# Second layer of a four-layer hybrid block: k projected two heads ahead, and a mixer's last three steps spread over ten steps of the gates

## The chip, the core and the metric

The kernel runs on one core of one Trainium2 chip. The core's engines run side by side and each takes its own instructions in order: TensorE (PE, matmuls; PEld is its weight load), VectorE (DVE), ScalarE (ACT), GpSimd (POOL) and SyncE (SP), which issues nearly all of the DMAs here. The metric is the device time of one execution in microseconds (us); less is better. Matmul results land in PSUM, 8 banks of 128 x 512 f32; everything else lives in SBUF.

## What is computed

Four layers over 1040 tokens (16 meta tokens and 1024 others) of width 1024: attention with a sliding window (layers 0 and 3), mLSTM (layer 1) and HGRN2 (layer 2). Each does RMS norm, an input projection, its mixer, a gate and an output projection that is added to the residual. The change is in the second layer alone (`kind == 1`). Cut to that layer:

```python
def mlstm_branch(u, w_in, conv_w, conv_b, gate_bias, h_gain, w_out, valid):
    q, k, v, ig, fg, og, z = _split(u @ w_in, B_SIZES)      # 8 heads, dk 128, dv 256
    qk = silu(causal_conv(concat([q, k]), conv_w, conv_b))  # 4 taps over the tokens
    ...
    h = mlstm_chunkwise(qh, kh * 128 ** -0.5, vh, log_i, log_f)   # blocks of 128 tokens
    h = sigmoid(og) * h
    h = rmsnorm(h, h_gain)                                  # per head
    return (h * silu(z)) @ w_out

def step(carry, inp):              # one head, one block of 128 tokens
    C, n, m = carry
    ...
    D = where(causal, a[t] - a[s] + li[s], -inf)
    qk = (q_ @ k_.T) * exp(D - m_t)
    num = w_inter * (q_ @ C) + qk @ v_
    den = w_inter * (q_ @ n) + qk.sum(-1)
    h = num / maximum(abs(den), exp(-m_t))
    C_new = w_old * C + (w_s * k_).T @ v_
```

## The kernel before

**Numbers.** Everything is f32 to its full precision: an operand is split into a high and a low part (`split`, lines 194 to 196: ACT rounds to fp32r at L195, DVE takes the rest at L196), and each product is three matmuls, high by high, high by low and low by high. Weights are fetched in two halves of 128 x 512 (`weights`, L207, on SP's queue) and split in the same way into the tiles `wh` and `wl`, of which there are three each; there are two raw landing tiles `wr`.

**Steps.** The program is one long list of steps, each `[cost, function, prefetch]`. The cost is in units near a nanosecond of ideal matmul time; it only serves to place steps. PE executes them exactly in the order of the list. The order on ACT, DVE, POOL and SP is made by the framework's scheduler from the order of the list and its own model of time; `hi(...)` lets a step's instructions go ahead of those listed up to 40 places earlier. A step's `prefetch` (the weights) is put out 12,000 units of cost ahead of the step (`LOOKAHEAD`). `weave(a, b)` mixes two lists so that both advance by the same share of their cost; `flat` strings lists together; `later` puts a step so many units behind a list's start.

**Projections.** `proj` (L231) makes one 128-wide piece of q, k, output gate `og` or gate `z` for all tokens: three chunks of 400, 384 and 256 tokens, four steps to a chunk, six matmuls to a step, so 72 matmuls. `proj_v` (L281, and L277 for the meta tokens) makes v of a head, block by block. `proj_out` (L326) multiplies a head's result by its output weights and adds to the residual `x` on DVE (L329). It first splits its input by `ysplit` steps of cost 0.

**What follows a chunk of q or k** (`conv_proj`): ACT copies PSUM to `t` (L956) and makes the last tap (L959), DVE adds three taps (L961), then a sigmoid (ACT L454, L455, L456, L458, DVE L457) and a product (DVE L965 or L967). q lives in a pool of two tiles, k in a row of the eight `r` rows, which it shares with the two result rows of each head.

**The mixer of a head** (`mixer`) has nine blocks b and four steps to a block. `s1(b)` (PE L1009, L1011): q by k, the decay matrix E on DVE (L1013, from rows `rw` fetched by SP at L990 one block ahead, three tiles) and ACT (L1015), W = E * qk (DVE L1019), splits of V, W, q and k. `s2(b)`: the numerator, W by V and q by the carried state (PE L997, `po<-Vh,Wh` and `po<-Ch,qwh`), then the division on ACT and DVE. `s3(b)`: the state's update (PE L997 `pa<-Vh,kwh`, DVE L1062 or L1064 into C, then C's split into Ch and Cl). `s4(b)`: the transpose of the result into the rows R["h"] (PE L1073, DVE L1075). The list of a mixer is s1(0); s1(1), s2(0), s3(0); s1(2), s2(1), s3(1), s4(0); and so on, with costs 320, 714, 357 and 214. Its last three steps, `rest`, are s2(8), s4(7) and s4(8).

**The order of the layer.** `body` starts with q0, k0, q1 and the gates' scalar rows. Then, for h = 0 to 5: the mixer of head h but for its last three steps, woven with q(h+1), k(h+1), v(h+1) (h = 0 has no q: q1 is done); `rest` woven with the first six steps of `gates(h)`; the other steps of `gates(h)`, which are og's two projections and the first of z's, with the norm's sums; z's second projection `zg[h][1]`; the output projection `oc[h]`. Mixer 6 is woven with q7, k7, v7, and mixer 7, headed by the three steps held back from mixer 6, follows at once with gates(6) and zg[6][1] beside it. Then come the rest of mixer 7 with gates(7), and zg[7][1]; oc[6] and oc[7] run beside the next layer's head.

Of the kernel before, what the change touches and what calls it, by code (L numbers as in the profile page):

```python
# [32 lines left out]

B_COLS = 96
LOOKAHEAD = 12000.0
TAIL_LAG = 600.0
PRIO = 40
ROWS, TMPS, RAWS, YS = 8, 6, 2, 3
# [19 lines left out]
def weave(a, b):  # L58

    ta, tb = sum(x[0] for x in a) + 1e-9, sum(x[0] for x in b) + 1e-9  # L60
    out, i, j, ca, cb = [], 0, 0, 0.0, 0.0
    while i < len(a) or j < len(b):
        if j >= len(b) or (i < len(a) and ca / ta <= cb / tb):
            ca += a[i][0]
            out.append(a[i])
            i += 1
        else:
            cb += b[j][0]
            out.append(b[j])
            j += 1  # L70
    return out


def flat(groups):
    return [x for grp in groups for x in grp]


def outs(groups):

    first, out = groups[0]  # L80
    out = list(out)
    for splits, grp in groups[1:]:
        out.insert(len(out) - Y_EARLY, splits[0])
        out.insert(len(out) - Y_LAST, splits[1])
        out += grp
    return first, out


def later(steps, *events):

    k, t = 0, 0.0
    for delay, step in events:
        while k < len(steps) and (t < delay or steps[k][0] == 0.0):
            t += steps[k][0]
            k += 1
        steps.insert(k, step)
        t += step[0]
        k += 1
# [15 lines left out]
def hybrid_kernel(ctx: ExitStack, tc: tile.TileContext, ins, out, layers=(0, 1, 2, 3)):  # L114
# [134 lines left out]
    def proj_v(srcs, evac, kind="v"):  # L249

        st = {}
        nc = 256 if kind == "v" else 272
        pieces, k = [], 0
        for src in srcs:
            n = src.shape[-1] // nc
            pieces.append((k, n, src))
            k += n

        groups = []
        for blocks in CHUNK_BLOCKS:  # L260
            grp = []
            for b in blocks:
                c0, cn = blk(b)
                for i, (k0, kn, src) in enumerate(pieces):
                    def pre(i=i, src=src):
                        st[i] = weights(src, kind)

                    def fn(b=b, c0=c0, cn=cn, i=i, k0=k0, kn=kn):
                        if i == 0:
                            st["a", b] = psj()  # L270
                        acc = st["a", b]
                        wh, wl = st[i]
                        for kk in range(kn):
                            k = k0 + kk
                            if b == 0:
                                for m in (wh, wl):
                                    pe.matmul(acc[:48, :nc], um[0][:, k, :], m[:, kk, :],  # L277
                                              start=(k == 0 and m is wh), stop=(k == KT - 1 and m is wl))
                            else:
                                for j, (a, m) in enumerate(((uh, wh), (uh, wl), (ul, wh))):  # L280
                                    pe.matmul(acc[:cn, :nc], a[:, k, c0 : c0 + cn], m[:, kk, :],  # L281
                                              start=(k == 0 and j == 0), stop=(k == KT - 1 and j == 2))
                        if i == len(pieces) - 1:
                            evac(acc, b, c0, cn)

                    grp.append([(2 if b == 0 else 3) * kn * nc * MM, fn, pre if b == 0 else None])
            groups.append(grp)
        return groups
# [172 lines left out]
    def gate_proj(src, o, chunks=CHUNKS, scale=None):  # L461
        rs = {}

        def early(n, c0, cn):
            rs[n] = tmp()
            scale.fetch(rs[n], c0, cn)

        def evac(acc, n, c0, cn):
            cs = slice(c0, c0 + cn)
            z = acc[:, :cn]  # L470
            if scale is not None:
                z = rs[n][:, :cn]
                v.tensor_tensor(z, z, acc[:, :cn], op=ALU.mult)
            a = sigmoid_from(z, cn)
            v.tensor_tensor(a[:, :cn], a[:, :cn], z, op=ALU.mult)
            v.tensor_tensor(o()[:, cs], o()[:, cs], a[:, :cn], op=ALU.mult)

        return proj(src, evac, chunks, None if scale is None else early)
# [384 lines left out]
    def layer_b(i, j, fin):  # L863
# [78 lines left out]
        def conv_proj(src, mt, mul, key):  # L942
            prev = [None, None]

            def evac(acc, n, c0, cn):
                conv = R["conv"]
                raw = tmp()
                if n == 0:
                    if mt < 8:
                        R[key] = R["mix"].tile([P, T], F32, tag="q", name=nm("q"), bufs=2)  # L950
                    else:
                        R[key] = row()
                    v.memset(raw[:, 0:3], 0.0)
                else:
                    v.tensor_copy(raw[:, 0:3], prev[0][:, prev[1] : prev[1] + 3])
                s.copy(raw[:, 3 : 3 + cn], acc[:, :cn])  # L956
                prev[:] = [raw, cn]
                y = R[key][:, c0 : c0 + cn]
                s.activation(y, acc[:, :cn], AF.Identity, bias=conv[:, mt, 4:5], scale=conv[:, mt, 3:4])  # L959
                for q in (2, 1, 0):  # L960
                    v.scalar_tensor_tensor(y, raw[:, q : q + cn], conv[:, mt, q : q + 1], y,  # L961
                                           op0=ALU.mult, op1=ALU.add)
                a = sigmoid_from(y, cn)
                if mul == 1.0:
                    v.tensor_tensor(y, y, a[:, :cn], op=ALU.mult)  # L965
                else:
                    v.scalar_tensor_tensor(y, y, mul, a[:, :cn], op0=ALU.mult, op1=ALU.mult)  # L967

            return proj(src, evac)

        def v_evac(h):
            def f(acc, b, c0, cn):
                R["v", h, b] = V = vtile()
                put_v(V, acc, b, cn)
                if h == 0:
                    gate_evac(acc, b, cn)
                g.memset(V[:cn, 256:258], 1.0)
            return f
# [110 lines left out]
        def og_proj(h):  # L1089
# [20 lines left out]
            def stat(n, c0, cn):  # L1110
                def fn():
# [6 lines left out]
                    for c in range(2):  # L1118
# [8 lines left out]
        qg = {h: conv_proj(win[8 * h], h, 1.0, ("q", h)) for h in range(8)}  # L1127
        kg = {h: conv_proj(win[8 * h + 1], 8 + h, 128 ** -0.5, ("k", h)) for h in range(8)}
        gsrc = [ins["b_wv0"][j][:, 272 * a : 272 * b] for a, b in ((0, 3), (3, 6), (6, 8))]
        vg = {h: proj_v([win[8 * h + 2], win[8 * h + 3]], v_evac(h)) if h else proj_v(gsrc, v_evac(0), "g") for h in range(8)}  # L1130
        og = {h: og_proj(h) for h in range(8)}
        zg = {h: [gate_proj(win[8 * h + 6 + c], lambda h=h, c=c: R["h", h, c]) for c in range(2)] for h in range(8)}
        oc = {h: proj_out(wout[2 * h], wout[2 * h + 1], lambda k, h=h: R["h", h, k], CHUNKS,
                          fin if h == 7 else None, h == 6) for h in range(8)}

        def gates(h):
            g0, g1, stats = og[h]
            tail = flat(zg[h][0])
            for n in (2, 1, 0):
                later(tail, (7000.0, stats[n]))  # L1140
                tail = g0[n] + g1[n] + tail
            return tail
# [5 lines left out]
        body = flat(qg[0]) + flat(kg[0]) + flat(qg[1])  # L1148
        later(body, (GATE_LAG, gate_turn(2)), (0.0, [0.0, gate_rows, None]), (GATE_COLS, [18 * 30, gate_cols, None]))
        for h in range(8):  # L1150
            mx = mixer(h)
            mx, rest = mx[:-3], mx[-3:]
            if h < 7:
                body += weave(mx, (flat(qg[h + 1]) if h else []) + flat(kg[h + 1]) + flat(vg[h + 1]))
                if h < 6:
                    body += weave(rest, gates(h)[:6]) + gates(h)[6:] + flat(zg[h][1]) + flat(outs(oc[h]))
                else:
                    held = rest
            else:
                body += weave(held + mx, gates(6) + flat(zg[6][1]))  # L1160
        body += weave(rest, gates(7)[:6]) + gates(7)[6:] + flat(zg[7][1])
        return head, body, oc[6], oc[7]

    def layer_c(i, j, fin):
# [288 lines left out]
        for h in range(8):  # L1453
# [11 lines left out]
            for r in range(1, 5):  # L1465
                mx += weave(main[r], last)
                last = [[TAIL_LAG, lambda: None, None]]
                if r == 1:
# [19 lines left out]
    for pos, i in enumerate(layers):  # L1488
# [10 lines left out]
        if i % 3 == 0:  # L1499
            head, body, oa, ob = layer_a(i, i // 3, tail is None, i == 3, fin, norm if tail is None else None)  # L1500
        elif i % 3 == 1:
            head, body, oa, ob = layer_b(i, i // 3, fin)
        else:
            head, body, oa, ob = layer_c(i, i // 3, fin)
# [42 lines left out]
    for n, (cost, fn, pre) in enumerate(steps):  # L1547
        while k < len(steps) and (k <= n or ahead < LOOKAHEAD):
            if steps[k][2]:
# [117 lines left out]
```

## Time and profile before

| | us |
|---|---|
| median of 3 runs | 2602.28 (2600.02 to 2602.58) |
| the profiled execution | 2599.31 |
| its span, first to last instruction | 2597.5 |
| PE busy in the span | 2541.0 |
| DVE busy | 2034.6 |
| ACT busy | 1744.6 |
| the second layer, from the first projection of q to the last steps of its gates | about 510 to 1530 |

Busy times are sums of records; a matmul's record lasts longer than the distance to the next one, so PE counts as busy from the first of a run of matmuls until the last has left the array. PEclk is the share of full clock that TensorE was granted. Waits are inferred from semaphores and name the last thing to arrive. A row of the timeline has start, duration, engine, line, operation, tiles, shapes and, in brackets, the idle time of that engine just before, with what ended it.

### The profile page before, as it was taken

What the parts mean: (1) busy time and instruction counts of PE and PEld (TensorE: products, weight loads), DVE (VectorE), ACT (ScalarE), POOL (GpSimd) and SP (SyncE); (2) the same over time, 40 slices, a digit from 0 to 9 for tenths busy, and PEclk for the clock granted to TensorE, in tenths of its full rate; (3) what the DMA queues carried; (4) which work ended last, traced back from release to release, by engine and by line L of the source; (5) the groups of instructions that cost most, each with busy time, mean ns of one, the idle gap of its engine ahead of it and who ended that gap; (6) DMA issues with size and microseconds to landing.
All of it is one profiled execution on the core that took longest, in us unless ns stands there. A gap on an engine that the chain in (4) does not pass through costs nothing.

```text
span 2597.5 us, 55485 instructions
## 1 busy us (share of the span) xinstructions
PE 2541.0 (98%) x20646; PEld 2488.2 (96%) x20646; DVE 2034.6 (78%) x5602; ACT 1744.6 (67%) x4675; POOL 244.2 (9%) x572
## 2 busy tenths in 40 slices
PE   8999999989999999999999999999999999999999
PEld 8899999989999999999999999999999998999999
DVE  7897898785757576767677788978888988887886
ACT  8766766576565656565657757877675857867772
POOL 0321231000000000000000000001000000321320
PEclk9999999999999999999999999999999999999999
DMA  5223212022222212121211111111111113212112
GB/s 157 63 66 94 57 43 69 30 51 56 43 50 45 52 46 53 45 50 49 50 49 43 55 43 43 34 34 34 34 42 34 35 51 93 64 47 77 56 42 77
DMA packets 103344, 140.27 MB, mean 54 GB/s; under 512 B 15369, under 2 KB 58514, under 8 KB 103074
## 3 DMA queue, kind: packets, MB, share of 16 engines
q1 hardware_dynamic: 103074, 136.73, 19.2%
q8 instruction: 162, 2.65, 0.4%
q14 instruction: 108, 0.88, 0.1%
HBM read 121.83 MB, written 4.27 MB: 49 GB/s over the span
## 4 chain that ended last, share of the span: by engine, by line
PE 61%; DVE 14%; ACT 9%; DMA 4%; issue 2%; SPq 0%; POOL 0%; DVEq 0%; ACTq 0%
PE pj L231 29%; PE pj L326 14%; PE pj L281 8%; DMA rw<-rowsd 2%; DVE wl L196 2%; PE po L997 1%; PE po L773 1%; PE pt L755 1%; ACT Sm L737 1%; DVE Sm L734 1%; ACT wh L195 1%; ACT X L1291 1%; PE pj L277 1%; PE pa L997 1%; DVE x L329 1%
## 5 line engine op out<-in xcount | busy, mean ns | idle before, releaser
L231 PE MATMUL pj<-uh,wh 128*128 128x256 f32 (+2 forms) x2688 | 903.6, 336 | 6.9 <-ACT uh L401 6.4
L231 PE MATMUL pj<-ul,wh 128*128 128x256 f32 (+2 forms) x2688 | 865.3, 322 | 0.3
L231 PE MATMUL pj<-uh,wl 128*128 128x256 f32 (+2 forms) x2688 | 864.9, 322 | 0.0
L231 PEld LDWEIGHTS pj<-uh,wh 128*128 128x128 f32 x2688 | 509.0, 189 | 14.6 <-ACT uh L401 6.4
L231 PEld LDWEIGHTS pj<-ul,wh 128*128 128x128 f32 x2688 | 509.4, 189 | 4.4 <-DVE ul L196 0.8
L231 PEld LDWEIGHTS pj<-uh,wl 128*128 128x128 f32 x2688 | 508.0, 189 | 0.0
L196 DVE TENSOR_TENSOR wl<-wr,wh 128x512 fp32r<-128x512 f32 (+1 forms) x338 | 234.2, 703 | 72.0 <-ACT wh L195 69.4
L326 PE MATMUL pj<-yh,wh 128*128 128x384 f32 (+2 forms) x768 | 253.4, 330 | 9.9 <-DVE x L329 8.3
L329 DVE TENSOR_TENSOR x<-x,pj 128x384 f32<-128x384 f32 (+2 forms) x480 | 233.9, 507 | 32.9 <-PE pj L326 31.7
L195 ACT CAST wh<-wr 128x512 fp32r<-128x512 f32 (+1 forms) x338 | 203.3, 614 | 78.7 <-PE pj L326 31.0
L326 PE MATMUL pj<-yh,wl 128*128 128x384 f32 (+2 forms) x768 | 246.3, 321 | 0.0
L326 PE MATMUL pj<-yl,wh 128*128 128x384 f32 (+2 forms) x768 | 246.3, 321 | 0.0
L281 PE MATMUL pj<-wh,uh 128*128 128x256 f32 (+1 forms) x768 | 222.8, 290 | 0.0
L281 PE MATMUL pj<-wl,uh 128*128 128x256 f32 (+1 forms) x768 | 216.3, 282 | 0.0
L281 PE MATMUL pj<-wh,ul 128*128 128x256 f32 (+1 forms) x768 | 215.9, 281 | 0.0
L737 ACT ACTIVATE Sm<-Sm,s 128x257 f32<-128x257 f32 (+2 forms) x272 | 131.1, 483 | 87.7 <-DVE s L734 85.2
L740 POOL TENSOR_TENSOR Sm<-Sm,s 128x512 f32<-128x512 f32 (+2 forms) x136 | 139.4, 1025 | 404.9 <-DVE s L739 389.6
L458 ACT ACTIVATE t<-t 128x384 f32<-128x384 f32 (+2 forms) x240 | 118.2, 493 | 64.5 <-DVE t L457 63.5
L195 ACT CAST yh<-r 128x384 fp32r<-128x384 f32 (+2 forms) x120 | 56.9, 478 | 154.8 <-PE pj L326 138.0
L326 PEld LDWEIGHTS pj<-yh,wh 128*128 128x128 f32 x768 | 144.7, 188 | 13.9 <-DVE x L329 10.4
L326 PEld LDWEIGHTS pj<-yl,wh 128*128 128x128 f32 x768 | 144.9, 189 | 0.7 <-DVE yl L196 0.2
L281 PEld LDWEIGHTS pj<-wh,uh 128*128 128x128 f32 x768 | 144.7, 188 | 0.6
(323 smaller groups left out, 5704.0 us busy)
## 6 DMA issues: line engine op xcount, KB each, us to landing
wr<-in_b_win SPq DMA_DIRECT2D x124, 256.0 KB, 2.8
wr<-in_a_win SPq DMA_DIRECT2D x80, 256.0 KB, 2.7
wr<-in_c_win SPq DMA_DIRECT2D x64, 256.0 KB, 3.0
wr<-in_a_wout SPq DMA_DIRECT2D x32, 256.0 KB, 2.8
rw<-rowsd SPq DMA_DIRECT2D x64, 128.0 KB, 4.3
wr<-in_b_wout SPq DMA_DIRECT2D x32, 256.0 KB, 2.8
t<-t SPq DMA_DIRECT2D x100, 48.0 KB, 1.9
cs<-in_rope SPq DMA_DIRECT2D x11, 400.0 KB, 3.5
```

Of the source, the lines that this page charges most:

```text
L195: s.copy(h, src)
L196: v.tensor_tensor(l, src, h.bitcast(F32), op=ALU.subtract)
L231: pe.matmul(acc[:, :cn], a[:, k, :], b[:, k, c0 : c0 + cn], start=(k == 0 and i == 0), stop=(k == KT - 1 and i == 2))
L277: pe.matmul(acc[:48, :nc], um[0][:, k, :], m[:, kk, :], start=(k == 0 and m is wh), stop=(k == KT - 1 and m is wl))
L281: pe.matmul(acc[:cn, :nc], a[:, k, c0 : c0 + cn], m[:, kk, :], start=(k == 0 and j == 0), stop=(k == KT - 1 and j == 2))
L326: pe.matmul(acc[:, :cn], a[:, k, mc], b, start=(k == 0 and i == 0), stop=(k == 1 and i == 2))
L329: v.tensor_tensor(x[:, m, c0 : c0 + cn], x[:, m, c0 : c0 + cn], acc[:, :cn], op=ALU.add)
L458: s.activation(a[:, :cn], a[:, :cn], AF.Exp)
L734: v.tensor_tensor_reduce(Sm[:nq, u, :nk], S[:nq, u, :nk], R["masks"][:nq, P + mo : P + mo + nk], rq, sinks[u], ALU.add, ALU.min, st[:nq, u ...
L737: s.activation(Sm[:nq, u, : nk + 1], Sm[:nq, u, : nk + 1], AF.Exp, scale=-1.0, bias=st[:nq, u : u + 1], accum_out=den[:nq, u : u + 1])
L740: g.tensor_tensor(Sm[:nq, :, :nk], Sm[:nq, :, :nk], den[:nq].rearrange("p (u c) -> p u c", c=1).to_broadcast([nq, 2, nk]), op=ALU.mult)
L997: pe.matmul(acc, a[x0], c[x1][:, :258], start=(start and i == 0), stop=(stop and i == 2))
```

## The change

Three things, all in `layer_b`. k of head h+2 takes the place of k of head h+1 beside mixer h; beside mixer 0 both k1 and k2 are projected, and beside mixer 6, where no k is left, z's second projection of head 5. That moves `zg[5][1]` from ahead of mixer 6 to beside it, and `oc[5]` from ahead of mixer 6 to behind it. The rest of a mixer is woven with the first ten steps of the gates, and an empty step of 600 units is put ahead of it, which does nothing but shift its place in the weave.

```diff
+REST_LAG, REST_STEPS = 600.0, 10
...
             if h < 7:
-                body += weave(mx, (flat(qg[h + 1]) if h else []) + flat(kg[h + 1]) + flat(vg[h + 1]))
+                fill = flat(qg[h + 1]) if h else flat(kg[1])
+                fill += flat(kg[h + 2]) if h < 6 else flat(zg[5][1])
+                body += weave(mx, fill + flat(vg[h + 1]))
                 if h < 6:
-                    body += weave(rest, gates(h)[:6]) + gates(h)[6:] + flat(zg[h][1]) + flat(outs(oc[h]))
+                    n, gs = REST_STEPS, gates(h)
+                    body += weave([[REST_LAG, lambda: None, None]] + rest, gs[:n]) + gs[n:]
+                    if h < 5:
+                        body += flat(zg[h][1]) + flat(outs(oc[h]))
                 else:
+                    body += flat(outs(oc[5]))
                     held = rest
             else:
                 body += weave(held + mx, gates(6) + flat(zg[6][1]))
-        body += weave(rest, gates(7)[:6]) + gates(7)[6:] + flat(zg[7][1])
+        n, gs = REST_STEPS, gates(7)
+        body += weave([[REST_LAG, lambda: None, None]] + rest, gs[:n]) + gs[n:] + flat(zg[7][1])
```

## The prediction

> **What bounds the kernel now.** I read the page's first part, then what PE waited for inside the second layer, then that layer cut into stages.
>
> ```profile
> PE 2541.0 (98%) x20646; PEld 2488.2 (96%) x20646; DVE 2034.6 (78%) x5602; ACT 1744.6 (67%) x4675; POOL 244.2 (9%) x572
> ```
> ```profile
> PE po L997 <- ACT Ch L195: 5.5, 5, 2.0
> PE po L997 <- DVE Cl L196: 3.6, 7, 1.1
> PE po L997 <- ACT Wh L195: 3.2, 1, 3.2
> PE po L997 <- DVE Wl L196: 0.4, 1, 0.4
> ```
> ```profile
> 541.00:570.00 29.00, 22.36 (x125) 21.11 (x124) 23.11 (x72) 22.61 (x62) 0.20 (x2) 0.82 0.13 32
> 570.00:596.00 26.00, 26.00 (x223) 26.00 (x221) 19.13 (x68) 16.14 (x54) 0.65 (x5) 1.00 0.23 42
> 596.00:612.00 16.00, 13.56 (x87) 13.11 (x86) 7.71 (x26) 6.69 (x20) 1.02 (x7) 0.89 0.49 74
> 676.00:729.00 53.00, 53.00 (x402) 52.80 (x401) 41.48 (x135) 36.07 (x105) 0.78 (x7) 1.00 0.32 53
> 729.00:744.00 15.00, 14.06 (x104) 13.62 (x103) 7.61 (x24) 6.90 (x20) 0.68 (x5) 1.00 0.48 64
> 862.00:877.00 15.00, 13.76 (x102) 13.35 (x102) 7.21 (x24) 7.04 (x20) 0.76 (x7) 1.00 0.30 62
> 995.00:1010.00 15.00, 14.39 (x106) 13.95 (x105) 7.70 (x25) 7.59 (x23) 0.68 (x5) 1.00 0.37 63
> 1127.00:1142.00 15.00, 14.44 (x107) 14.00 (x106) 7.94 (x25) 7.17 (x21) 0.86 (x7) 1.00 0.35 63
> 1259.00:1275.00 16.00, 15.72 (x116) 15.43 (x116) 8.66 (x27) 8.67 (x23) 1.34 (x10) 1.00 0.35 72
> 1391.00:1406.00 15.00, 14.99 (x112) 14.45 (x112) 8.80 (x30) 7.76 (x22) 0.55 (x3) 1.00 0.25 79
> 1406.00:1460.00 54.00, 54.00 (x374) 53.81 (x373) 44.63 (x143) 44.94 (x127) 0.00 (x0) 1.00 0.15 48
> ```
>
> PE sets the time: 2541.0 of 2597.5 us busy. The change removes no matmul, so it can only win where PE stands still. In the second layer all such waits are of one line, s2's products (12.7 us in 14 waits), and the stages place them. The first number of a row is its length and the second PE's busy time. Mixer 0's first blocks (541 to 570) lose 6.64 us at a granted clock of 0.82. The ends of mixers 0 to 5 lose 2.44, 0.94, 1.24, 0.61, 0.56 and 0.28, together 6.07. The body of mixer 1 (676 to 729) loses nothing, nor does the end of mixer 6 or mixer 7.
>
> How a run of matmuls really goes, and so what a step costs, is in its starts, not its durations:
>
> ```profile
> 533.90 0.34 PE L231 MATMUL pj<-ul,wh 128*128 128x400 f32 x1
> 534.08 0.35 PE L231 MATMUL pj<-uh,wl 128*128 128x400 f32 x1
> ...
> 596.39 0.28 PE L281 MATMUL pj<-wl,uh 128*128 128x256 f32 x1
> 596.51 0.28 PE L281 MATMUL pj<-wh,ul 128*128 128x256 f32 x1
> ```
> ```profile
> 549.31 4.00 PE pj L231 x12
> 560.69 3.52 PE pj L231 x12
> 639.89 14.33 PE pj L231 x96
> ```
>
> A 400 column matmul takes 0.18 us of PE, one of 256 columns 0.12. The 96 matmuls of the last piece are a projection (72) and a chunk of 256 (24), so a projection is 14.33 - 24 x 0.12 = 11.45 us. A record outlasts its slot by 0.16 us (0.28 - 0.12), so each wait is longer by that than the windows show. In mixer 0, 12 matmuls that should take 2.2 us took 4.00 and 3.52: 1.8 + 1.3 us lost to the lowered clock. Mixer 0's start thus costs 6.64 + 4 x 0.16 + 3.1 = **10.4 us**. The ends cost 6.07 + 10 x 0.16 = 7.7, plus up to 0.11 x 16 = 1.8 of clock behind mixer 0: **7.7 to 9.4 us**.
>
> **Part 1: the rest of a mixer is spread.** Why an end stalls, shown at mixer 2:
>
> ```profile
> 869.36 0.35 DVE L1013 SCALAR_TENSOR_TENSOR E<-rw,bcol,caus 128x128 f32<-128x128 f32 x1 [2.99 <-DMA rw<-rowsd]
> 869.63 0.48 DVE L1064 SCALAR_TENSOR_TENSOR C<-C,rw,pa 128x258 f32<-128x258 f32 x1
> ...
> 870.28 1.14 ACT L195 CAST wh<-wr 128x512 fp32r<-128x512 f32 x2
> ...
> 871.32 0.41 ACT L195 CAST Ch<-C 128x258 fp32r<-128x258 f32 x1
> ...
> 871.78 0.39 PE L997 MATMUL po<-Ch,qwh 128*128 128x258 f32 x1 [0.79 <-ACT Ch L195]
> ...
> 872.14 0.42 DVE L196 TENSOR_TENSOR Cl<-C,Ch 128x258 fp32r<-128x258 f32 x1
> ...
> 872.62 0.39 PE L997 MATMUL po<-Cl,qwh 128*128 128x258 f32 x1 [0.45 <-DVE Cl L196]
> ```
>
> On DVE the update of C stands behind an E that waits 2.99 us for its row's DMA, and on ACT C's cast stands behind two weight casts. s2(8) is the next thing on PE's list after the last of the mixer, so PE waits. In the new weave the empty step is 600 of 600 + 714 + 214 + 214 = 34% of the list. Ten steps of the gates are 8 x 1000 + 2 x 960 units, and three of them are 30%, four 40%: s2(8) comes behind four steps, which are a whole chunk, 24 x 0.18 = 4.4 us of PE. The largest end stall is 2.44 + 0.32, so the cover suffices at all six ends. s4(7) and s4(8) follow the eighth and ninth step; who reads them last is og's third chunk, which starts behind the sixteenth, so nothing new is late. PE's work and its order beyond are the same, and no DMA is moved. Bounds: 3 us, if the scheduler lets the gates' own work into ACT and DVE ahead of C and half or more of the wait comes back; 9.4 at most. I take **8.5**, near the upper end, because the cover is larger than every wait.
>
> **Part 2: k2 beside mixer 0.** What is late at its start:
>
> ```profile
> 545.10 0.15 DVE L1019 TENSOR_TENSOR W<-E,pm 16x16 f32<-16x16 f32 x1
> ...
> 545.55 0.47 ACT L956 COPY t<-pj 128x400 f32<-128x400 f32 x1
> ...
> 547.21 0.29 ACT L195 CAST Wh<-W 128x128 fp32r<-128x128 f32 x1
> ...
> 555.98 0.42 DVE L1062 COPY C<-pa 128x258 f32<-128x258 f32 x1
> ...
> 558.16 0.40 ACT L195 CAST Ch<-C 128x258 fp32r<-128x258 f32 x1
> ```
>
> The copy at 545.55 is that of q1's first chunk, whose 400 column matmuls ended on PE at 534.4: ACT and DVE run 11 us behind with the convolutions of k0 and q1. W is ready at 545.25 and its cast comes at 547.21, behind that work; C, at 555.98, is cast at 558.16.
>
> The mixer's list is 12,946 units without its rest. s2(0) stands at 640 of them (4.9%), s3(0) at 1354 (10.5%), s2(1) at 2031 (15.7%). The fill grows by one projection, 11.45 us, so s2(0) moves back by 0.56 us, and between s3(0) and s2(1) there is 5.2% x 11.45 = 0.60 us more. That alone takes 1.2 us off the two stalls. During k1 only k2's weights are now prepared, where before both pieces of v1 were:
>
> ```profile
> L196 DVE TENSOR_TENSOR wl<-wr,wh 128x512 fp32r<-128x512 f32 (+1 forms) x338 | 234.2, 703 | 72.0 <-ACT wh L195 69.4
> L195 ACT CAST wh<-wr 128x512 fp32r<-128x512 f32 (+1 forms) x338 | 203.3, 614 | 78.7 <-PE pj L326 31.0
> ```
>
> Two halves fewer are 1.2 us of ACT and 1.4 of DVE out of the queues that are late: 1.2 more. Of the 3.1 us of clock I credit a third, 1.1, since the first gap only shrinks. Bounds for the start: nothing (the queues stay as late), and all 10.4. I take **3.5**, nearer the lower bound, because the backlog itself is not touched.
>
> [...]
>
> What k2 puts back: its own three chunks of convolution on ACT and DVE while they are still late. Lower bound nothing: mixer 1 with q, k and v beside it, the very same mix, loses nothing in 53 us. Upper bound is the slower rival below. I take **-1**, near mixer 1's row. Its two weight DMAs join SP's queue ahead of some `rw` fetches; mixer 1 carries the same load, so nothing is added.
>
> **Part 3: the seams.** Later k's keep the shape of their mixers, k is only a head older, and at most six of the eight rows are held (h5 twice, h6 twice, k6, k7). Beside mixer 6 the lighter zg[5][1] stands for k7. Mixer 6 now follows gates(5) at once; mixer 7 followed mixer 6 at once before, at 0.01 us lost, so 0. oc[5] now follows mixer 6, and its first product needs two splits from queues that are late by a mixer's end: 0 to 1.24 us (the ends of mixers 1 to 5), I take **-0.5**. Its second half of weights must wait for v7 to leave a `wh` tile: two casts and a subtraction, 2 x 0.61 + 0.70 = 1.9 us, hidden by the eight products ahead of it, 24 x 0.18 = 4.4 us; uncovered it would cost those 1.9.
>
> **Sum.** 8.5 + 3.5 - 1 - 0.5 = 10.5 us. Against the profiled execution's own 2599.31 (its span is 2597.5) that is 2588.8; the runs' median stands 3.0 us above that execution, so 2602.28 - 10.5 = **2592**. The bounds of the terms that remain likely give it 2587 to 2597.
>
> **The rivals.**
> - *Only the ends gain.* The start's stalls stay whole, since the backlog is what sets them: 8.5 - 0.5 = 8, 2594.5. For it: W waits on ACT's queue, not on PE's order. Against: two weight splits leave that queue.
> - *Mixer 0 heals wholly*, as mixers 1 to 5 run without a loss: 8.5 + 10.4 = 19, 2583. Against: those start behind an output projection, with empty queues.
> - *No change that can be measured.* ACT and DVE are ordered by the scheduler, not by the weave, and it was this order that put an E and weight casts ahead of C; it may do so again with the gates' work. The ends then give 3, the start 1.2, and the seams take 1.2 and 1: 2 us, 2600.
> - *Slower.* The 11 us of lag does not drain, since k1 and k2 together bring six chunks of convolution, and blocks 2, 3 and 4 of mixer 0 stall as block 1 did (2.0 + 1.1 of wait, 0.3 of records, 1.3 of clock: 4.7 each). The ends gain 8.5, the start nothing, the seams lose 0.5: 3 x 4.7 - 8 = 6 us, 2608. It decides from the second such block on. Against it: from 570 to 596 mixer 0 loses nothing, at closer steps than the change gives it.
>
> **Chances.** Forecast 0.45, only the ends 0.14, healed 0.13, no change 0.16, slower 0.12. About 0.2%, 5.2 us, is what a measurement of this kernel can tell from no change: faster 0.72, same 0.16, slower 0.12. The range, 2583 to 2602, leaves out the slower case and the far end of the healed one.
>
> **What would show it.** Waits of `po` on Ch and Cl at the ends of mixers 0 to 5 should be gone (6.07 us of idle under 1), with s2(8) behind a chunk of L231. Mixer 0's first 29 us should lose 3 to 6 us instead of 6.64 and the stretch with k2 under 2; the steps of mixer 0 should come as evenly as those of mixer 1. The seams show as idle before oc[5]'s first L326. The prediction is wrong if the ends still wait, or if mixer 0 loses more than now.

## The result and the profile after

The changed kernel takes 2585.14 us (median of 6 runs, 2580.66 to 2586.18), the kernel before 2598.73 in its six runs by now. The ratio is 0.9943, with a 95% interval of 0.993 to 0.9956: 14.8 us less by the ratio, 13.6 by the medians. The forecast was 10.5 us less. The profiled execution took 2586.18 us against 2599.31, 13.1 less.

The chain of work that ended last brackets the second layer by the output projections of the layer before it and its own, which run beside the next layer's head. First column start, second length in us. Before:

```profile
451.75 20.51 PE pj L326 x141
...
1531.37 20.44 PE pj L326 x140
```

After (all lines of the code are one or a few higher):

```profile
454.66 20.52 PE pj L327 x141
...
1519.19 20.42 PE pj L327 x140
```

From one to the other it is 1079.62 us before and 1064.53 after: the second layer is 15.1 us shorter, and the untouched first layer happened to end 2.9 us later in this execution. Totals of work are as before:

```profile
PE 2536.4 (98%) x20646; PEld 2486.1 (96%) x20646; DVE 2034.8 (79%) x5602; ACT 1740.8 (67%) x4675; POOL 244.5 (9%) x572
```

The layer cut into stages, with mixer 0's first blocks, its later ones, its end, the end of mixer 1, and the seam of mixer 6 with oc[5] behind it (length, then PE's busy time; the third number from the right is the granted clock):

```profile
541.00:570.00 29.00, 23.86 (x149) 22.74 (x148) 24.12 (x71) 23.61 (x63) 0.20 (x2) 0.94 0.15 42
570.00:606.00 36.00, 36.00 (x289) 35.84 (x288) 29.83 (x99) 26.44 (x79) 0.58 (x5) 1.00 0.22 45
606.00:622.00 16.00, 16.00 (x112) 15.96 (x111) 6.69 (x21) 7.26 (x20) 0.68 (x5) 1.00 0.46 76
...
733.00:748.00 15.00, 15.00 (x117) 15.00 (x116) 7.36 (x26) 5.96 (x19) 1.06 (x8) 1.00 0.44 41
...
1303.00:1370.00 67.00, 67.00 (x506) 66.80 (x505) 49.57 (x156) 43.62 (x126) 1.03 (x9) 1.00 0.21 48
1370.00:1396.00 26.00, 26.00 (x169) 25.66 (x168) 17.70 (x44) 6.96 (x18) 0.31 (x1) 1.00 0.18 61
```

What PE still waited for in the layer, but for one wait of 0.2 us in a norm (us in total, times, longest):

```profile
PE po L998 <- ACT Wh L196: 2.1, 1, 2.1
PE po L998 <- ACT Ch L196: 1.7, 1, 1.7
PE po L998 <- DVE Cl L197: 0.7, 1, 0.7
PE po L998 <- DVE Wl L197: 0.7, 1, 0.7
```

All waits at the ends are gone, the four at mixer 0's start are left (5.2 us where 6.7 were), k2's stretch and both seams lose nothing. The clock's mean in the first 29 us rose from 0.82 to 0.94. Windows miss what a matmul's record covers, 0.16 us of each wait, so I also summed, for every matmul, its distance to the next start above the median distance of its line, tiles and width: 541 to 570 us went from 12.2 to 8.3, the end of mixer 0 from 4.5 to 0.2, and all from 612 to 1540 from 14.8 to 8.5. That is 14.6 of the 15.1 us.

Why the ends no longer wait, at mixer 0 in the timeline after:

```profile
610.96 0.35 DVE L1014 SCALAR_TENSOR_TENSOR E<-rw,bcol,caus 128x128 f32<-128x128 f32 x1 [2.70 <-DMA rw<-rowsd]
611.23 0.48 DVE L1065 SCALAR_TENSOR_TENSOR C<-C,rw,pa 128x258 f32<-128x258 f32 x1
...
612.92 0.41 ACT L196 CAST Ch<-C 128x258 fp32r<-128x258 f32 x1
...
613.74 0.42 DVE L197 TENSOR_TENSOR Cl<-C,Ch 128x258 fp32r<-128x258 f32 x1
...
616.75 0.28 PE L998 MATMUL po<-Vh,Wh 128*128 128x258 f32 x1
...
617.23 0.28 PE L998 MATMUL po<-Cl,qwh 128*128 128x258 f32 x1
```

The queue is not cured: E still holds DVE for 2.70 us in front of C. But Cl is ready at 614.16 and its product comes at 617.23, 3.1 us later, because og's first chunk, 24 matmuls from 612.26 on, now stands ahead of s2(8).

### The profile page after: what moved, and what is told of

The parts are those of the page before. It is cut to its first block, busy times and chain, and to the rows that moved or that the text cites. A ratio compares the mean times of both kernels' runs of the same rounds, so it can differ in the third digit from the quotient of the medians.

```text
span 2584.4 us, 55470 instructions
## 1 busy us (share of the span) xinstructions
PE 2536.4 (98%) x20646; PEld 2486.1 (96%) x20646; DVE 2034.8 (79%) x5602; ACT 1740.8 (67%) x4675; POOL 244.5 (9%) x572
## 4 chain that ended last, share of the span: by engine, by line
PE 61%; DVE 14%; ACT 10%; DMA 2%; issue 2%; SPq 0%; POOL 0%; DVEq 0%; ACTq 0%; POOLq 0%
PE pj L232 27%; PE pj L327 14%; PE pj L282 9%; PE po L998 2%; DVE wl L197 1%; ACT Sm L738 1%; DVE Sm L735 1%; PE po L774 1%; PE pt L756 1%; PE pa L998 1%; ACT X L1299 1%; ACT wh L196 1%; PE pj L278 1%; DVE x L330 1%; DVE X L1297 1%
## 5 line engine op out<-in xcount | busy, mean ns | idle before, releaser
L232 PE MATMUL pj<-uh,wh 128*128 128x384 f32 (+2 forms) x2688 | 903.8, 336 | 6.7 <-ACT uh L402 6.2
L232 PE MATMUL pj<-ul,wh 128*128 128x384 f32 (+2 forms) x2688 | 864.9, 322 | 0.3
L232 PE MATMUL pj<-uh,wl 128*128 128x384 f32 (+2 forms) x2688 | 864.4, 322 | 0.0
L232 PEld LDWEIGHTS pj<-uh,wh 128*128 128x128 f32 x2688 | 508.6, 189 | 14.6 <-ACT uh L402 6.5
```

The lines of the kernel that those rows point to most:

```text
L232: pe.matmul(acc[:, :cn], a[:, k, :], b[:, k, c0 : c0 + cn], start=(k == 0 and i == 0), stop=(k == KT - 1 and i == 2))
```

## The experiments

All ratios are to the kernel before, with 95% intervals; the changed kernel has 0.9943. An interval is 5.7 to 7.8 us wide, so ratios alone do not tell most of these kernels from the changed one. The length of the second layer in the trace, taken between the same two matmuls as in the section above, is free of what the other layers add. It is one execution of each kernel, so differences of a few tenths say nothing:

| run | second layer, us | less than before |
|---|---|---|
| before | 1079.6 | |
| the changed kernel | 1064.5 | 15.1 |
| only the spread | 1070.0 | 9.6 |
| only the order of k | 1071.5 | 8.2 |
| ten steps, no empty step | 1071.4 | 8.2 |
| seams left | 1065.1 | 14.6 |
| mixer 0: 1200 and 1000 units | 1062.1 | 17.5 |
| fewer taps | 1059.7 | 19.9 |
| mixer 0: 2200 units ahead | 1064.1 | 15.5 |
| two subtractions on GpSimd | 1067.0 | 12.7 |
| rows in four pieces | 1066.5 | 13.1 |
| the same, with 900 and 600 units | 1065.2 | 14.5 |
| 900 and 600 units alone | 1065.8 | 13.8 |

### Each part alone

Only the spread of the rest (the kernel before, with `weave([[REST_LAG, lambda: None, None]] + rest, gs[:n]) + gs[n:]` at both places):

> Only the rest of a mixer is spread (empty step of 600, ten steps of the gates); k, zg[5][1] and oc[5] stay where they were. Theory A (the two parts add up; the ends are worth about 10 us by the trace, 6.07 us of idle with the records' overlap and the clock behind mixer 0): 9 to 10.5 us under the kernel before, ratio near 0.9963, no wait of L997's line at the ends, mixer 0's start as before (6 to 7 us idle in 541 to 570). Rival B (the longer fill of mixer 0 is what relieved mixer 0's end): the end of mixer 0 still waits 2 us, 5 to 6 us gained, ratio 0.998.

Measured: **0.9959** (0.9946 to 0.9971), 10.7 us by the ratio, 9.6 by the layer's length. Waits of PE in the layer, but for one of 0.3 us in a norm:

```profile
PE po L998 <- ACT Wh L196: 3.1, 1, 3.1
PE po L998 <- ACT Ch L196: 1.8, 1, 1.8
PE po L998 <- DVE Cl L197: 1.1, 1, 1.1
PE po L998 <- DVE Wl L197: 0.4, 1, 0.4
```

One of each: these are mixer 0's first blocks, as in the kernel before. All six ends are healed by the spread alone, mixer 0's too, so theory A holds and rival B falls.

Only the order of k, zg[5][1] and oc[5]:

```diff
-REST_LAG, REST_STEPS = 600.0, 10
+REST_LAG, REST_STEPS = 600.0, 6
...
-body += weave([[REST_LAG, lambda: None, None]] + rest, gs[:n]) + gs[n:]
+body += weave(rest, gs[:n]) + gs[n:]
```

> Only the order of k, zg[5][1] and oc[5]; the rest of a mixer is woven with six steps of the gates and no empty step, as before. Theory A: mixer 0's start gains 3 to 4 us, the ends of mixers 0 to 5 still wait 0.3 to 2.4 us each; 4 us under before, ratio near 0.9985. Rival B: mixer 0's end heals too, with 8 us under before, ratio 0.997. Rival C (k2 costs beside mixer 0 what it gains): ratio 1.000.

Measured: **0.9971** (0.996 to 0.9982), 7.5 us by the ratio, 8.2 by the layer's length: rival B's size. In the waits neither text holds whole. The start has the changed kernel's waits, and the ends still wait, as theory A has it. At the end of mixer 0, 603 to 615 us:

```profile
PE po L998 <- ACT Ch L196: 0.6, 1, 0.6
PE po L998 <- DVE Cl L197: 0.5, 1, 0.5
```

where before it was 2.0 and 0.5 us with a clock of 0.89. With k2 beside it, mixer 0's end is like that of any other mixer. By the layer's length the two parts alone make 17.7 us and together 15.1. The 2.6 us that are in both are mixer 0's end: summed by distances between starts, as above, it loses 4.5 us in the kernel before and 1.8 here. Beside the spread the order of k is thus worth 5.5 us by the layer's length, and 4.1 by the ratios, whose intervals overlap.

### Which part of the spread carries it

The changed kernel without the empty step: `weave(rest, gs[:n])`, ten steps of the gates kept.

> The changed kernel without the empty step of 600 units: ten steps of the gates, but s2(8) stays the first thing behind the mixer. Theory A (the cover is the chunk of og ahead of s2(8), and the number of steps is nothing): the ends wait as before, time as the kernel with k alone, ratio to before near 0.9985. Rival: the wider spread of s4(7) and s4(8) carries part of the gain: 0.996.

Measured: **0.9965** (0.9952 to 0.9978), the same as with k alone. The number is the rival's, but the kernel with k alone, from which theory A took its own, came out lower than forecast too. The waits at the ends are back, seven on Cl where one was left:

```profile
PE po L998 <- ACT Ch L196: 3.5, 4, 1.7
PE po L998 <- DVE Cl L197: 3.3, 7, 0.7
...
```

`weave` takes the first list's first step before anything else, so without the empty step s2(8) stays right behind the mixer, whatever the number of gate steps. By the layer's length ten steps without the empty one are worth 0.1 us over the order of k alone, so the spread works through the empty step. An empty step with only six steps of the gates was not run.

### The seams

zg[5][1] and oc[5] left ahead of mixer 6:

```diff
-fill += flat(kg[h + 2]) if h < 6 else flat(zg[5][1])
+fill += flat(kg[h + 2]) if h < 6 else []
...
-if h < 5:
-    body += flat(zg[h][1]) + flat(outs(oc[h]))
+body += flat(zg[h][1]) + flat(outs(oc[h]))
...
-body += flat(outs(oc[5]))
 held = rest
```

> The changed kernel with zg[5][1] and oc[5] left ahead of mixer 6, so that mixer 6 has only q7 and v7 beside it. Theory A (a mixer behind an output projection starts with empty queues, and its fill's length is nothing): as the changed kernel, within 1 us, ratio to before 0.9945. Rival (a mixer with two projections fewer beside it runs its steps too close, as mixer 0 did before): 4 to 10 us slower than the changed kernel, with waits on Wh, Ch and Cl in mixer 6, ratio 0.996 to 0.998.

Measured: **0.9942** (0.993 to 0.9954). The only wait in mixers 6 and 7 is one of 0.5 us on Cl. For a mixer that stands behind an output projection, a fill shorter by a projection costs nothing here; this move is neutral. That empty queues are the reason, as theory A says, was not measured.

### What sets mixer 0's start

More distance, with empty steps in mixer 0 alone, ahead of s2(1) and of s2(0):

```diff
+if h == 0:
+    mx.insert(6, [1000.0, lambda: None, None])
+    mx.insert(3, [1200.0, lambda: None, None])
```

> The changed kernel with two empty steps in mixer 0 alone: 1200 units ahead of s2(0), 1000 ahead of s2(1), so that s2(0) comes 3.4 us and s2(1) another 2.8 us of fill later. Theory P (the start's stalls are a matter of distance: s1(0) to s2(0) and s3(0) to s2(1) are shorter than the late queues' answer): the two waits (2.1 + 0.7 and 1.7 + 0.7 us) and the half clock go, 5.5 to 7 us under the changed kernel, ratio to before near 0.992. Rival Q (the queues of ACT and DVE are late and only a standing PE lets them catch up): the waits come back at s2(1) and s2(2), at most 2 us gained, ratio 0.9935 to 0.9945.

Measured: **0.9937** (0.9925 to 0.9949), not to be told from the changed kernel by the ratio; the layer is 2.4 us shorter. The layer's waits:

```profile
PE po L998 <- DVE Cl L197: 1.7, 4, 0.6
PE po L998 <- ACT Ch L196: 0.7, 1, 0.7
PE pm L1010 <- DVE kwl L1035: 0.4, 1, 0.4
...
PE pj L282 <- ACT v L248: 0.3, 1, 0.3
```

The two long waits and the half clock (0.51 in the changed kernel) went (1.00 from 541 to 606 us), as theory P has it, but small waits came at later blocks, as Q has it: 3.1 us in mixer 0 instead of 5.2. The gain is near Q's 2 us and not P's 5.5 to 7.

Less backlog: q0, k0 and q1 without two of the three earlier taps of their convolution (`for q in (2,)` in place of `(2, 1, 0)`), so that their values differ.

> The changed kernel without two of the three earlier taps of the convolution for q0, k0 and q1, which are the three projections ahead of mixer 0: 18 instructions of DVE of about 0.55 us, 9.9 us less in the late queue. If that backlog sets the start's stalls (both theories P and Q say it does, in different ways), the waits of mixer 0's first blocks fall from 5.1 us to under 1.5 and the time is 4 to 7 us under the changed kernel, ratio to before 0.992 to 0.993. Rival R (it is the chain of mixer 0 itself, E, W, its cast and the product, that is too slow for its distance, backlog or not): the waits stay, ratio 0.994 to 0.9945.

Measured: **0.9925** (0.991 to 0.9939), 4.7 us under the changed kernel; the intervals overlap, but the layer is 4.8 us shorter too. One wait is left in mixer 0, 1.6 us on Wh. How late the queues are can be read from ACT's copies of a projection's first chunk: q0's, some 0.4 us behind the end of its matmuls, and q1's, the last before mixer 0. The changed kernel:

```profile
513.41 0.47 ACT L957 COPY t<-pj 128x400 f32<-128x400 f32 x1
...
548.43 0.47 ACT L957 COPY t<-pj 128x400 f32<-128x400 f32 x1
```

and with fewer taps:

```profile
512.01 0.47 ACT L957 COPY t<-pj 128x400 f32<-128x400 f32 x1
...
542.05 0.48 ACT L957 COPY t<-pj 128x400 f32<-128x400 f32 x1
```

35.0 us apart against 30.0: five us less late, as the matmuls of the two chunks lie 24.2 us apart in both. 3.6 us of the start's 5.2 us of waits and the half clock are gone (1.00 from 541 to 606 us). The backlog sets most of the start; rival R falls.

The whole mixer later, one empty step of 2200 units ahead of it (`mx.insert(0, ...)`):

> The changed kernel with one empty step of 2200 units ahead of all of mixer 0: the whole mixer begins 6.9 us of fill later, the distances between its steps are a little shorter than in the changed kernel. Theory P (distance between s1(0) and s2(0), and s3(0) and s2(1), against late queues): the same waits some 7 us later, 5 us of wait, time as the changed kernel or up to 1 us more, ratio 0.994 to 0.995. Rival (a later start meets queues that have caught up): the waits go, ratio 0.992.

Measured: **0.9951** (0.9936 to 0.9966). In mixer 0:

```profile
PE po L998 <- ACT Wh L196: 1.7, 1, 1.7
PE po L998 <- ACT Ch L196: 1.3, 2, 0.7
PE po L998 <- DVE Cl L197: 1.1, 3, 0.4
PE po L998 <- DVE Wl L197: 0.5, 1, 0.5
...
```

4.6 us of the same waits, later, though without the half clock (1.00 from 541 to 606 us). That 6.9 us more of fill do not let the queues catch up, with k1's convolution coming in meanwhile, is the likely reading.

Two subtractions of the gates' scalar rows on GpSimd (`g.tensor_tensor` for `bs` and `a`):

> The changed kernel with two subtractions of the gates' scalar rows (2 x 1.22 us of DVE at 523 to 527) on GpSimd, which is idle there. Theory S (the rows' chain of nearly 9 us on DVE ahead of the convolutions is where the lateness comes from): the queues are up to 2.4 us less late, the start's waits fall by 1 to 2.5 us, ratio to before near 0.9935. Rival (GpSimd needs longer for the two than DVE, and the exponentials on ACT behind them wait): no gain or a loss of 1 to 2 us, ratio 0.9945 to 0.995.

Measured: **0.9958** (0.9946 to 0.997), 4 us slower than the changed kernel by the ratios, whose intervals overlap, and 2.4 by the layer's length. q1's first copy comes 14.2 us behind the end of its matmuls, where it was 11.1 in the changed kernel: the queues are later, and the rival holds, with a larger loss than it said. The rows of GpSimd and DVE show more than it said:

```profile
525.04 2.62 POOL L917 TENSOR_TENSOR r<-r,r 8x1040 f32<-8x1040 f32 x1 [24.15 <-DVE r L915]
525.29 2.39 DVE L956 COPY t<-t 128x3 f32<-128x3 f32 x1
527.61 0.67 DVE L197 TENSOR_TENSOR wl<-wr,wh 128x512 fp32r<-128x512 f32 x1
527.74 3.82 POOL L918 TENSOR_TENSOR r<-r,r 8x1040 f32<-8x1040 f32 x1
528.21 0.55 DVE L966 TENSOR_TENSOR q<-q,t 128x400 f32<-128x400 f32 x1
528.70 0.60 DVE L962 SCALAR_TENSOR_TENSOR q<-t,bcols,q 128x384 f32<-128x384 f32 x1
529.22 2.88 DVE L197 TENSOR_TENSOR wl<-wr,wh 128x512 fp32r<-128x512 f32 x1
```

GpSimd takes 2.62 and 3.82 us where DVE took 1.22 each, and one DVE instruction beside each is held up until GpSimd is done, at 527.66 and 531.56: a copy of three columns takes 2.39 us, to 527.68, a weight's split 2.88, to 532.10. Not all are: at 528.21 and 528.70 two run at their usual length within GpSimd's second row, which is itself 1.2 us longer than the first.

The rows' chain listed in four pieces instead of one, so that q0's first chunk is listed ahead of the scans:

```diff
-(0.0, [0.0, gate_rows, None])
+(0.0, [0.0, rows_sig, None]), (4500.0, [0.0, rows_max, None]),
+(6500.0, [0.0, rows_sum, None]), (8200.0, [0.0, rows_out, None])
```

> The changed kernel with the gates' scalar rows listed in four pieces (sigmoid at 2000 units as now, running maximum at 4500, block sums at 6500, the rest at 8200) instead of one, so that q0's first chunk of convolution is listed ahead of the scans. No instruction more or less. Theory S (the lateness starts where q0's convolution waits in the queues behind the rows' chain): q1's first copy comes 2 to 3 us sooner, mixer 0's start waits 2 to 3 us less, ratio to before 0.993 to 0.9935. Rival (the rows are what mixer 0 needs first, and they come later): E and W are later, 1 to 3 us more of wait, ratio 0.995 or above.

Measured: **0.9961** (0.9948 to 0.9973), the rival's number; mixer 0 waits 6.1 us. The two copies are as far apart as they were, 34.9 us:

```profile
510.14 0.47 ACT L963 COPY t<-pj 128x400 f32<-128x400 f32 x1
...
545.03 0.47 ACT L963 COPY t<-pj 128x400 f32<-128x400 f32 x1
```

Theory S's step failed: another place in the list does not make the queues less late. Whether the rows' chain is where the lateness comes from is not settled by it.

The same with smaller empty steps in mixer 0 (900 and 600 units), and these steps alone:

> As e9 with smaller empty steps in mixer 0, 900 units ahead of s2(0) and 600 ahead of s2(1). If lateness and distance both count, the two first waits go and what comes back later is under 3 us, as the queues are less late: 5 us under the changed kernel, ratio 0.9925. If only the lateness counts: as e9.

> The changed kernel with the smaller empty steps alone (900 and 600 units). From e5, where the first waits went and about 6 us of small ones came later: the first waits fall to under 1 us, and the later ones are fewer than in e5 since its steps lie less close; 2 to 3 us under the changed kernel, ratio 0.9935. Rival (the late queues take the same sum of waits wherever they fall): as the changed kernel, 0.9943.

Measured: **0.995** (0.9938 to 0.9962) and **0.9958** (0.9944 to 0.9971). Neither forecast gain came. The first still waits 5.7 us in mixer 0. In the second, mixer 0 waits:

```profile
PE po L998 <- ACT Ch L196: 2.2, 2, 2.0
PE po L998 <- DVE Cl L197: 2.2, 2, 1.7
PE po L998 <- DVE C L1065: 0.8, 1, 0.8
PE po L998 <- DVE Wl L197: 0.7, 1, 0.7
```

5.9 us, partly at other blocks. Against the changed kernel's 5.2 us, empty steps in mixer 0 left 5.9, 4.6 and, with the largest distances, 3.1: they move the waits and take at most part of them away. Of the variants that leave no work out, none is clearly faster than the changed kernel by its ratio.

## Why the prediction was right, point by point

**The ends (8.5 us forecast).** Right in mechanism. The waits on Ch and Cl at all six ends went, for the reason given, a chunk of og ahead of s2(8); without the empty step they return (0.9965). Alone the spread is worth 9.6 us by the layer's length, just above the upper bound of 9.4; its ratio says 10.7, with an interval from 7.5 to 14.0. The bound of 3 us, the scheduler giving half of it back, did not come about: C stands where it stood in the queues.

**Mixer 0's start (3.5 us).** Right in size, 2.9 us by the windows (idle 6.64 to 5.14, and at most 1.7 lost in one stretch of half clock where 3.1 were) and 3.9 by the distances. The split was otherwise: the waits gave 1.5 us where I had 2.4, the clock 1.4 or more where I had 1.1. How much of it is more distance between the steps and how much the two weight halves fewer, no run separates. The reason for staying near the lower bound, that the backlog is not touched, is what the runs with fewer taps (0.9925) and with more distance (0.9937, waits moved on) support.

**k2's own work (-1 us) and the seams (-0.5 us).** Both cost nothing: 36.00 of 36 us busy with k2 beside mixer 0, 67.00 of 67 and 26.00 of 26 around mixer 6 and oc[5]. The row I had for it, mixer 1's 53 us without a loss, was the better guide than the caution added to it.

**The sum.** 10.5 us against 13.6 to 14.8 by the runs and 15.1 by the layer. The ends were put 1.1 us too low. The order of k was put lower still: its terms, 3.5 - 1 - 0.5, make 2 us, and beside the spread it is worth 5.5 by the layer's length. Of these 3.5 us more, 1.5 are the two charges that did not come, 0.4 the start by the distances, and 1.4 lie from 622 us on by the same sums. About 1 us of that is small waits of s2's products on Ch and Cl, 0.3 us at most, which the spread alone still has inside later mixers and the changed kernel has not. The forecast has no term for these. Nor has it one for k2 relieving mixer 0's end, 2.7 us with k alone; it is luck that this did no harm to the sum, since the spread covers that end anyway.

**The rivals.** "Only the ends gain" has the larger part right, 9.6 of the 15.1 us, but not the start, which fell from 6.7 to 5.2 us of waits. "Heals wholly" fails at the four waits left. By size neither its 19 us nor the 8 of the first is close. "Slower" would have needed waits from block 2 on; there are none in 570 to 606. "No change" needed the gates' work to hold C back; at mixer 0 Cl is ready 2.9 us after the start of C's update, 2.7 before, and the chunk of og covers it.

## What to carry to other kernels

PE runs a fixed order here and waited for a short chain on other engines. It was enough to list that chain's consumer 24 matmuls later, behind work that was ready; the queue that makes it late was not mended (E still held DVE for 2.70 us). Check that the weave really moves it: a list's first step goes first, and it took an empty step, not a longer partner list, to do it. At mixer 0's start, where the queues themselves run 11 us late, moving consumers mostly moved the waits: of 5.2 us, 5.9, 4.6 and 3.1 were left in three tries.

## What the runs showed of the hardware

**DVE was held up beside GpSimd.** With a GpSimd subtraction of 8 x 1040 beside it, DVE's copy of 128 x 3 took 2.39 us and a 128 x 512 subtraction 2.88; in the changed kernel the same instructions, one after the other, take

```profile
526.48 0.15 DVE L956 COPY t<-t 128x3 f32<-128x3 f32 x1
526.55 0.67 DVE L197 TENSOR_TENSOR wl<-wr,wh 128x512 fp32r<-128x512 f32 x1
```

Two other DVE instructions, of 128 x 400 and 128 x 384, ran in 0.55 and 0.60 us in the first 1.6 us of GpSimd's longer row. What sets them apart from the two that were held up, the trace does not show.

**The clock fell behind one pair of gaps and not behind the other.** Around mixer 0's start in the changed kernel:

```profile
546.80:553.00 6.20, 3.46 (x20) 2.92 (x19) 5.58 (x18) 5.11 (x15) 0.00 (x0) 1.00 0.15 44
557.00:560.20 3.20, 0.80 (x5) 0.39 (x3) 3.15 (x10) 2.87 (x8) 0.10 (x1) 1.00 0.00 0
560.20:563.60 3.40, 3.40 (x14) 3.40 (x15) 2.50 (x11) 2.77 (x9) 0.00 (x0) 0.51 0.00 0
```

2.74 us idle in the first stretch, in gaps of 2.1 and 0.7 us, went with a clock of 1.00; 2.40 in the second, shorter one, in gaps of 1.7 and 0.7, were followed by 3.4 us at 0.51. In the kernel before, both pairs had a lowered clock behind them: gaps of 3.2 and 0.4 us, with 12 matmuls in 4.00 us at 0.50, and of 2.0 and 1.1, with 12 in 3.52 at 0.57. So of the two stretches of lowered clock one is gone. What tells the two pairs apart, no run here shows.
